# Mixer B's score products: three float32r passes against two 16-bit passes and a half-array remainder

## The chip, the cores and the metric

The kernel runs on one core of one Trainium2 chip, in one launch. The metric is the device time of that launch in microseconds: the median of three runs of the kernel before is 2332.86 us (2331.59 to 2336.87). One further execution, whose time is 2334.11 us, was recorded by the hardware profiler; all rows below are from it.

## The reference

An encoder block over 2048 tokens of width 1024: a norm, one input projection, two attention mixers side by side (A: dilated windows; B: latent attention), an output projection, a mixture of experts, a final norm. All of it is float32. The change is in mixer B, which computes for each of 8 heads

```python
q = (rmsnorm(c_q, g_q_latent) @ w_q_up).reshape(b, s, 8, 64 + 32)     # 64 "nope", 32 rotary
kv = (rmsnorm(c_kv, g_kv_latent) @ w_kv_up).reshape(b, s, 8, 64 + 64) # k_nope, v
k_r = apply_rope(k_rope)                                              # one rotary key for all heads
sc = (q_nope . k_nope + q_rope . k_r) * 96 ** -0.5                    # 2048 x 2048 per head
p = softmax(sc); o = p @ v
```

So each score is a dot product over 96 numbers, of which the last 32 of the key are the same in all heads.

## The kernel before

The block runs in stages on one core: projections (to about 400 us of the span), mixer A (to 703 us), mixer B's preparation (`mla_prep`, 703 to 763 us), mixer B's loop (`mla`, 763 to 1524 us), then output projection, routing and experts.

float32 accuracy on the matrix engine is made by splitting each operand into a high part (float32r, rounded) and a low part (the rest), and adding three products: high x high, high x low, low x high. Each product reads 96 rows of the array (97 where a row with minus the query's maximum rides along) and 512 columns.

`mla` walks over 256 steps `s`: 8 heads x 4 blocks of 512 queries (`m`) x 8 pairs of 128 keys (`kp`). For one step PE does, in this written order: three score products of the first 128 keys (`scores(s, 0)`, L837 to L839), one product of a maximum pass that runs ten steps ahead (`maxpass`, L811, reduced by DVE in L813), three score products of the second 128 keys, another maximum-pass product. After every second step the values of two steps are multiplied in (`pv`, L868 to L873, 36 short float16 products). Now and then comes `mrow` (L821, L822: the finished maxima turned into a row of Qh) or one piece of the next head's k or q (`prep`, L792 to L799; both use the one PSUM bank `X`). ACT takes the exponential of a step's scores twice (L844 to float16 `hi`, L845 to float32 `p32`); their difference `lo` is made by DVE on the first LV = 256 of 512 columns (L850) and by POOL on the rest (L851). The score bank `S` has two buffers, the maximum-pass bank `M` two.

All engines run their queues in program order; the order is written out in the loop `for s in range(NS + 2)`. From step 194 on `ahead5` adds work of the next stage to the same queues, by step number.

`mla_prep` makes, per 128 tokens, the normed latents, q, v, and head 0's k and q. `krows` puts the rotary key into Kh and Kl, which POOL copies for the odd heads' buffers. `pre4` (in mixer A's last units) and `split_c` (in `phase1`) split weights.

Of the kernel before, what the change touches and what calls it, by code (L numbers as in the profile page):

```python
# [12 lines left out]
F32 = mybir.dt.float32  # L13
F32R = mybir.dt.float32r
F16 = mybir.dt.float16
# [7 lines left out]
S, D = 2048, 1024  # L23
# [13 lines left out]
class K:  # L37
# [23 lines left out]
    def consts(self, ctx):  # L61
        nc, tc, io = self.nc, self.tc, self.io
        self.cp = ctx.enter_context(tc.tile_pool(name="consts", bufs=1))
        self.ident = self.cp.tile([128, 128], F32, name="ident")
        make_identity(nc, self.ident)
        self.css = self.cp.tile([128, 2, NT], F32, name="css")
        self.vbs = self.cp.tile([128, 2], F32, name="vb_scale")
        self.RF = self.cp.tile([128, 68], F32, name="rf")
        self.idx = self.cp.tile([128, E], I32, name="eidx")
        self.novf = self.cp.tile([128, 1], I32, name="novf")  # L70
        self.idx2 = self.cp.tile([128, 6], I32, name="eidx2")
        self.glat = self.cp.tile([128, 3], F32, name="glat")
        self.ones = self.cp.tile([128, 128], F32, name="ones")
        nc.gpsimd.memset(self.ones, 1.0)


    def phase1(self):
# [3 lines left out]
        with ExitStack() as ctx:  # L81
# [96 lines left out]

            def split_c(h):
                split(wcv[0][:, 4 * h:4 * h + 4], wcv[1][:, 4 * h:4 * h + 4], wraw[h])  # L180

            stage_a(0)
            split_c(0)
# [37 lines left out]
            def vscale():  # L221

                am = sm.tile([128, 4], F32, name="vmax")
                for i in range(2):
                    nc.scalar.activation(hT[0][:, :, 1792:], raws[i].rearrange("p (j n) -> p j n", j=8), AF.Square, accum_out=am[:, i:i + 1])
                    yield
                nc.vector.tensor_reduce(am[:, 2:3], gb, axis=AX.X, op=ALU.max, apply_absolute_value=True)
                yield
                yield from self.pow2_scale(sm, pt, am, float(D), vsc, dr["va_inv"])

# [205 lines left out]
    def pre4(self, step):  # L436

        nc, io = self.nc, self.io
        f = lambda t: t[:, 0:1536].rearrange("p (k n) -> p k n", k=2)
        if step == 0:  # L440
            self.wq = [f(self.pre.tile([128, S], F32R, name=n)) for n in ("QA16", "KA")]
            self.wqraw = f(self.pre.tile([128, S], F32R, name="KB").bitcast(F32))
            nc.sync.dma_start(self.wqraw, io["w_q_up"][0].rearrange("(k p) n -> p k n", p=128))
            nc.sync.dma_start(self.glat[:, 0:2], io["g_q_latent"][0].rearrange("(k p) -> p k", p=128))
            nc.sync.dma_start(self.glat[:, 2:3], io["g_kv_latent"].rearrange("a p -> p a"))
        else:

            k = step - 1
            g = self.glat[:, k:k + 1]
            nc.scalar.activation(self.wq[0][:, k], self.wqraw[:, k], AF.Copy, scale=g)  # L450
            nc.vector.scalar_tensor_tensor(self.wq[1][:, k], self.wqraw[:, k], g, self.wq[0][:, k],
                                           op0=ALU.mult, op1=ALU.subtract)
# [292 lines left out]
                        put(h // 2, {3: 16, 11: 1, 19: 4}[u])  # L745


    def mla(self):
        nc, tc, io, dr = self.nc, self.tc, self.io, self.dram
        SC = 96 ** -0.5  # L750
        LN64 = math.log(64.0)
        LV = 256
        PASS = ((0, 0), (0, 1), (1, 0))
        with ExitStack() as ctx:
            self.open5()
            pq = ctx.enter_context(tc.tile_pool(name="p4q", bufs=1))
            pp = ctx.enter_context(tc.tile_pool(name="p4", bufs=1))

            names = ("Qh", "Ql", "Kh", "Kl")
            QK = [{n: self.slot(i) for i, n in enumerate(names)}, {n: pq.tile([128, S], F32R, name=n) for n in names}]  # L760
# [5 lines left out]
            sm = ctx.enter_context(tc.tile_pool(name="p4sm", bufs=2))  # L766
            with ExitStack() as c2:
                self.mla_prep(c2, SC, PASS, VB, ckvT, wkv, QK, vsc)
            self.c_pre.close()

            wk = ctx.enter_context(tc.tile_pool(name="p4w", bufs=3))
# [13 lines left out]
            def prep(h, i):  # L785
# [4 lines left out]
                if i % 2 == 0:  # L790
                    for n, (a, b) in enumerate(PASS):
                        nc.tensor.matmul(ps, wkv[b][:, h], ckvT[a][:, sl], start=(n == 0), stop=(n == 2))  # L792
                    nc.scalar.activation(d["Kh"][0:64, sl], ps[0:64], AF.Copy)
                    nc.vector.tensor_sub(d["Kl"][0:64, sl], ps[0:64], d["Kh"][0:64, sl])
                else:
                    for j in range(4):
                        nc.tensor.transpose(ps[0:96, 128 * j:128 * j + 128], qraw[h][:, 4 * n4 + j], self.ident)
                    nc.scalar.activation(d["Qh"][0:96, sl], ps[0:96], AF.Copy, scale=SC)
                    nc.vector.scalar_tensor_tensor(d["Ql"][0:96, sl], ps[0:96], SC, d["Qh"][0:96, sl],  # L799
                                                   op0=ALU.mult, op1=ALU.subtract)  # L800

            def maxpass(m, i):

# [7 lines left out]
                nc.tensor.matmul(ps, d["Qh"][0:96, q0:q0 + 128], d["Kh"][0:96, kc * 512:kc * 512 + 512],  # L811
                                 start=True, stop=True)
                nc.vector.tensor_reduce(part[m][:, qt, kc:kc + 1], ps, axis=AX.X, op=ALU.max)  # L813
                if kc == 3:
# [2 lines left out]
            def mrow(m):  # L817
                h, n = divmod(m, 4)
                ps = psX.tile([128, 512], F32, name="X")
                for qt in range(4):  # L820
                    nc.tensor.transpose(ps[0:97, 128 * qt:128 * qt + 128], mz[m % 2][:, qt], self.ident)  # L821
                nc.vector.tensor_scalar(QK[h % 2]["Qh"][96:97, n * 512:n * 512 + 512], ps[96:97], -1.0, LN64,  # L822
                                        op0=ALU.mult, op1=ALU.add)

            state = {}

            def scores(s, j):
# [6 lines left out]
                ps = state[s][0]  # L834
                k0 = (2 * kp + j) * 128
                kt = slice(k0, k0 + 128)
                nc.tensor.matmul(ps[:, j], d["Kh"][0:97, kt], d["Qh"][0:97, sl], start=True, stop=False)  # L837
                nc.tensor.matmul(ps[:, j], d["Kh"][0:96, kt], d["Ql"][0:96, sl], start=False, stop=False)
                nc.tensor.matmul(ps[:, j], d["Kl"][0:96, kt], d["Qh"][0:96, sl], start=False, stop=True)  # L839
                if j == 1:  # L840
                    hi = wk.tile([128, 2, 512], F16, name="hi", bufs=4)
                    p32 = wk.tile([128, 2, 512], F32, name="p32")
                    lo = wk.tile([128, 2, 512], F16, name="lo", bufs=4)
                    nc.scalar.activation(hi, ps, AF.Exp)  # L844
                    nc.scalar.activation(p32, ps, AF.Exp)  # L845
                    state[s] = (hi, lo, p32)

            def lows(s):
# [70 lines left out]
                    pv(s - 3)  # L919
                    pv(s - 2)  # L920

    def mla_prep(self, ctx, SC, PASS, VB, ckvT, wkv, QK, vsc):
# [15 lines left out]
        calls.update(enumerate(self.c4))  # L938
        nc.gpsimd.memset(kr[:, :, 0:64], 0.0)
        nc.sync.dma_start(kr[:, :, 64:96], AP(dr["c"], 384, [[416, 128], [128 * 416, NT], [1, 32]]))  # L940
        nc.scalar.activation(wkv[0], raw2, AF.Copy, scale=gkv)
        nc.vector.scalar_tensor_tensor(wkv[1], raw2, gkv, wkv[0], op0=ALU.mult, op1=ALU.subtract)
        rs = self.css
# [51 lines left out]
            nc.vector.scalar_tensor_tensor(VB[:, c, :, 65:129], v, vsc, VB[:, c, :, 0:64], op0=ALU.mult, op1=ALU.subtract)  # L995

        def krows(n4):
            ps = pt.tile([128, 4, 128], F32, name="pT")
            for j in range(4):
                nc.tensor.transpose(ps[0:96, j], kr[:, 4 * n4 + j], self.ident)  # L1000
            sl = slice(512 * n4, 512 * n4 + 512)
            src = ps[64:96].rearrange("p a b -> p (a b)")
            d = QK[0]
            nc.scalar.activation(d["Kh"][64:96, sl], src, AF.Copy)
            nc.vector.tensor_sub(d["Kl"][64:96, sl], src, d["Kh"][64:96, sl])
            for n in ("Kh", "Kl"):
                nc.gpsimd.tensor_copy(QK[1][n][64:96, sl], d[n][64:96, sl])

        def kprep(n4):
            sl = slice(512 * n4, 512 * n4 + 512)  # L1010
# [4 lines left out]
            nc.scalar.activation(QK[0]["Kh"][0:64, sl], pf[0:64], AF.Copy)  # L1015
            nc.vector.tensor_sub(QK[0]["Kl"][0:64, sl], pf[0:64], QK[0]["Kh"][0:64, sl])

        def qprep(c):
            if c % 4 == 0:
# [1 line left out]
            ps = qss["ps"]  # L1021
            nc.tensor.transpose(ps[0:96, c % 4], qss.pop(c)[:, 0, 0], self.ident)
            if c % 4 == 3:
                sl = slice(128 * (c - 3), 128 * (c + 1))
                pf = ps.rearrange("p a b -> p (a b)")
                nc.scalar.activation(QK[0]["Qh"][0:96, sl], pf[0:96], AF.Copy, scale=SC)
                nc.vector.scalar_tensor_tensor(QK[0]["Ql"][0:96, sl], pf[0:96], SC, QK[0]["Qh"][0:96, sl],
                                               op0=ALU.mult, op1=ALU.subtract)

        for c in range(2):  # L1030
            stage_a1(c)
        stage_a2(0)
        for c in range(NT):
            if c + 2 < NT:
# [4 lines left out]
            if c >= 1:  # L1039
                qprep(c - 1)  # L1040
            if c == 2:
                for d in QK:
                    nc.gpsimd.memset(d["Kh"][96:97].bitcast(F32), 1.0)
            if c in (4, 6, 8, 10):
                krows(c // 2 - 2)
            if c % 4 == 3:
# [1242 lines left out]
```

## Time and profile before

| | us |
|---|---|
| median of 3 runs | 2332.86 |
| the profiled execution | 2334.11 |
| its span (first to last instruction) | 2332.3 |
| PE busy in the span | 2132.7 (91%) |
| DVE / ACT / POOL busy | 1636.1 / 1361.2 / 1089.9 |
| mixer B's loop, 763 to 1524 us | 761 |

A matmul's record runs from its start to the modelled end of its last column, so records of neighbours overlap: a product is told by the distance from its start to the next one's start, not by its duration. PEld is the loading of weights, which overlaps with PE. The granted clock is a share of 2.4 GHz: 1.00 is the higher level, 0.50 the lower one (1.2 GHz), and values between are means over both.

### The profile page before, as it was taken

How to read it: one execution, taken by the hardware profiler on the slowest of the kernel's cores; microseconds unless marked ns; L12 is line 12 of the kernel's file. 1: busy time of each engine (PE TensorE's matmuls, PEld its weight loads, DVE VectorE, ACT ScalarE, POOL GpSimd, SP SyncE). 2: the span in 40 equal slices, each digit the busy share in tenths (PEclk: the TensorE clock that was granted, in tenths of full speed). 3: DMA queues.
4: the chain of work that ended last, by engine and by line, in shares of the span. 5: the costliest groups of instructions: out<-in, count | busy, mean ns of one | idle time of the engine just before them, and what ended most of it. 6: DMA issues, size and time to landing. Idle time of an engine off the chain costs nothing. (4 is left out here: it accounts for less than half of the span.)

```text
span 2332.3 us, 42859 instructions
## 1 busy us (share of the span) xinstructions
PE 2132.7 (91%) x16077; PEld 1805.7 (77%) x16077; DVE 1636.1 (70%) x3584; ACT 1361.2 (58%) x2103; POOL 1089.9 (47%) x1169
## 2 busy tenths in 40 slices
PE   6899998799999999999999999888888899999990
PEld 5899876699988688888888877776776588788870
DVE  7722111478887788888888898867787677777765
ACT  4522111588887477777777767734433366677653
POOL 1100000366673255555555556654664666667740
PEclk9999999889999899999999999999999999999995
DMA  4312536999955100000000131145534699899978
GB/s 163 126 60 81 193 161 173 208 220 204 206 129 155 36 20 22 6 22 6 22 22 6 27 119 26 34 135 157 153 128 173 195 305 293 292 306 321 307 211 305
DMA packets 196676, 333.79 MB, mean 143 GB/s; under 512 B 64185, under 2 KB 140898, under 8 KB 180388
## 3 DMA queue, kind: packets, MB, share of 16 engines
q1 hardware_dynamic: 166420, 195.41, 29.8%
q0 software_dynamic: 29760, 134.85, 18.0%
q8 instruction: 128, 2.10, 0.4%
q14 instruction: 80, 0.66, 0.1%
q10 hardware_dynamic: 288, 0.79, 0.1%
HBM read 248.24 MB, written 109.64 MB: 153 GB/s over the span
## 5 line engine op out<-in xcount | busy, mean ns | idle before, releaser
L851 POOL TENSOR_TENSOR lo<-p,hi 128x512 f16<-128x512 f32 x256 | 353.5, 1382 | 310.4 <-ACT p L845 308.1
L844 ACT ACTIVATE hi<-S 128x1024 f16<-128x1024 f32 x256 | 261.9, 1023 | 199.1 <-PE S L839 198.9
L813 DVE TENSOR_REDUCE part<-M 128x1 f32<-128x512 f32 x512 | 346.3, 685 | 32.5 <-PE M L811 30.5
L845 ACT ACTIVATE p<-S 128x1024 f32<-128x1024 f32 x256 | 261.0, 1019 | 0.2 <-DVE lo L850 0.2
L850 DVE TENSOR_TENSOR lo<-p,hi 128x512 f16<-128x512 f32 x256 | 218.1, 853 | 7.0 <-ACT p L845 0.2
L873 PE MATMUL O<-VB,lo 128*128 128x65 f16 x2048 | 197.6, 193 | 6.9 <-DVE lo L850 4.6
L868 PEld LDWEIGHTS <-hi 128*128 128x128 f16 x2048 | 182.7, 98 | 24.8 <-issue 23.2
L868 PE MATMUL O<-VB,hi 128*128 128x129 f16 (+1 forms) x2048 | 198.3, 215 | 0.0
L644 POOL TENSOR_TENSOR pp<-sb,st 128x512 f32<-128x512 f32 x32 | 33.5, 1049 | 327.6 <-DVE st L627 312.7
L873 PEld LDWEIGHTS <-lo 128*128 128x128 f16 x2048 | 177.3, 99 | 8.1 <-DVE lo L850 5.4
L650 POOL TENSOR_TENSOR pp<-sb,st 128x256 f32<-128x256 f32 (+1 forms) x256 | 143.0, 580 | 58.7 <-DVE st L627 49.4
L1994 DVE TENSOR_TENSOR s<-raw,s 128x1024 fp32r<-128x1024 f32 x120 | 140.0, 1220 | 16.0 <-ACT s L1992 15.8
L2038 POOL DMA_INDIRECT d_x<-o,rec x47 | 93.5, 1989 | 101.2 <-ACT s L1992 30.7
L1951 PE MATMUL pd<-s,hT 128*128 128x512 f32 x540 | 138.3, 404 | 1.7 <-ACT hT L1938 1.7
L307 DVE SCALAR_TENSOR_TENSOR qk_sb<-pm,qkscale,qk_sb 128x512 fp32r<-128x512 f32 x32 | 24.0, 751 | 163.2 <-ACT qk_sb L306 156.9
L1302 PE MATMUL pm<-s,mT_hi 128*128 128x512 f32 x512 | 134.3, 408 | 0.3 <-ACT mT_hi L1287 0.3
L1992 ACT ACTIVATE s<-raw 128x1024 fp32r<-128x1024 f32 x120 | 118.6, 1051 | 12.5 <-DMA raw<-in_w_gate,eidx 6.0
L1951 PEld LDWEIGHTS pd<-s,hT 128*128 128x128 f32 x540 | 101.0, 188 | 30.3 <-issue 4.3
L602 PE MATMUL S<-KA,QA 128*128 128x256 f32 (+2 forms) x384 | 114.5, 323 | 7.6 <-issue 7.6
L678 ACT ACTIVATE phi<-PT 128x512 f16<-128x512 f32 (+1 forms) x160 | 96.4, 602 | 39.9 <-PE PT L667 38.4
L306 ACT ACTIVATE qk_sb<-pm,qkscale 128x512 fp32r<-128x512 f32 x32 | 22.0, 688 | 167.2 <-DMA d_qk<-qk_sb 115.1
L1302 PEld LDWEIGHTS pm<-s,mT_hi 128*128 128x128 f32 x512 | 96.9, 195 | 21.9 <-ACT mT_hi L1287 0.5
(468 smaller groups left out, 6369.8 us busy)
## 6 DMA issues: line engine op xcount, KB each, us to landing
x<-in_x SPq DMA_DIRECT2D x32, 512.0 KB
d_qk<-qk_sb SPq DMA_DIRECT2D x64, 256.0 KB
na<-d_na SPq DMA_DIRECT2D x48, 264.0 KB
QA<-d_qk SPq DMA_DIRECT2D x16, 512.0 KB
KA<-d_qk SPq DMA_DIRECT2D x16, 512.0 KB
KB<-d_qk SPq DMA_DIRECT2D x16, 512.0 KB
d_x<-x SPq DMA_DIRECT2D x16, 512.0 KB
d_h<-h SPq DMA_DIRECT2D x16, 512.0 KB
```

The source lines that it names most:

```text
L650: nc.gpsimd.tensor_sub(dst, src, res[:, s0 + i, 65:66, None, None].to_broadcast([128, 2, na, nx // 2]))
L813: nc.vector.tensor_reduce(part[m][:, qt, kc:kc + 1], ps, axis=AX.X, op=ALU.max)
L844: nc.scalar.activation(hi, ps, AF.Exp)
L845: nc.scalar.activation(p32, ps, AF.Exp)
L850: nc.vector.tensor_sub(lo[:, :, 0:LV], p32[:, :, 0:LV], hi[:, :, 0:LV])
L851: nc.gpsimd.tensor_sub(lo[:, :, LV:512], p32[:, :, LV:512], hi[:, :, LV:512])
L868: nc.tensor.matmul(o[:, c0:c0 + own], hi[:, j, q], V[:, 0:own], start=(kt == 0 and qt == 0), stop=False, skip_group_check=True)
L873: nc.tensor.matmul(o[:, c0:c0 + 65], lo[:, j, q], V[:, 0:65], start=False, stop=(kt == 15 and qt == 3), skip_group_check=True)
L1302: nc.tensor.matmul(ps[half], mT[a][:, j], wo[b][j // 2][:, j % 2, 512 * half:512 * half + 512], start=(n == 0), stop=(n == 23))
L1951: self.nc.tensor.matmul(ps[:, half], hT[a][:, j], w[b][:, j, 512 * half:512 * half + 512], start=(n == 0), stop=(n == len(k) - 1))
L1992: nc.scalar.activation(hi, src, AF.Copy)
L1994: eng.tensor_sub(lo, src, hi)
```

## The change

q and k of mixer B become float16 high and low halves, after scaling by powers of two that are worked out at run time from sums of squares (`qk_scales`; the squares are summed by added `Square` activations in `split_c`, `pre4` and `mla_prep`). The rows are packed anew:

- K1 (128 rows): k_nope high, k_r high, k_r low; Q1: q_nope high, q_r high, q_r high again. Their product holds three of the terms.
- K2: k_nope low, k_nope high; Q2: q_nope high, q_nope low.
- K3, Q3 (33 rows, kept twice, at partitions 0 and 64): k_r high with q_r low, and a row that carries the maximum. The products of a step's two key tiles use the two halves of the array's rows.

The maximum pass multiplies Q1 and K1 in float16. The copies between partitions are DMAs on SP's queue (one per k piece, five per q piece, five per `krows`); POOL's copies go. The exponential takes its scale and bias from tiles. `mrow` now writes the maxima twice, by DVE and by ACT. LV goes from 256 to 192, so that DVE makes 384 and POOL 640 of a step's 1024 `lo` columns.

```diff
-                nc.tensor.matmul(ps[:, j], d["Kh"][0:97, kt], d["Qh"][0:97, sl], start=True, stop=False)
-                nc.tensor.matmul(ps[:, j], d["Kh"][0:96, kt], d["Ql"][0:96, sl], start=False, stop=False)
-                nc.tensor.matmul(ps[:, j], d["Kl"][0:96, kt], d["Qh"][0:96, sl], start=False, stop=True)
+                nc.tensor.matmul(ps[:, j], d["K1"][:, kt], d["Q1"][:, sl], start=True, stop=False)
+                nc.tensor.matmul(ps[:, j], d["K2"][:, kt], d["Q2"][:, sl], start=False, stop=False)
                 if j == 1:
+                    for i in range(2):
+                        r = slice(64 * i, 64 * i + 33)
+                        nc.tensor.matmul(ps[:, i], K3[r, k0 - 128 + 128 * i:k0 + 128 * i], d["Q3"][r, sl],
+                                         start=False, stop=True)
...
-                    nc.scalar.activation(hi, ps, AF.Exp)
-                    nc.scalar.activation(p32, ps, AF.Exp)
+                    nc.scalar.activation(hi, ps, AF.Exp, scale=es, bias=self.ln64)
+                    nc.scalar.activation(p32, ps, AF.Exp, scale=es, bias=self.ln64)
...
-        LV = 256
+        LV = 192
...
-                nc.vector.tensor_scalar(QK[h % 2]["Qh"][96:97, n * 512:n * 512 + 512], ps[96:97], -1.0, LN64,
-                                        op0=ALU.mult, op1=ALU.add)
+                q3 = QK[h % 2]["Q3"][:, n * 512:n * 512 + 512]
+                nc.vector.tensor_scalar(q3[32:33], ps[96:97], -2.0 ** -15, None, op0=ALU.mult)
+                nc.scalar.activation(q3[96:97], ps[96:97], AF.Copy, scale=-2.0 ** -15)
...
+    def put_q(self, d, ps, sl):
+        nc, sq = self.nc, self.mls[0:96, 0:1]
+        nc.scalar.activation(d["Q1"][0:96, sl], ps[0:96], AF.Copy, scale=sq)
+        ql = self.qlp.tile([128, 512], F16, name="ql")
+        nc.vector.scalar_tensor_tensor(ql[0:96], ps[0:96], sq, d["Q1"][0:96, sl], op0=ALU.mult, op1=ALU.subtract)
+        nc.sync.dma_start(d["Q2"][0:64, sl], d["Q1"][0:64, sl])
+        nc.sync.dma_start(d["Q1"][96:128, sl], d["Q1"][64:96, sl])
+        nc.sync.dma_start(d["Q2"][64:128, sl], ql[0:64])
+        nc.sync.dma_start(d["Q3"][0:32, sl], ql[64:96])
+        nc.sync.dma_start(d["Q3"][64:96, sl], ql[64:96])
...
         for c in range(2):
             stage_a1(c)
+        self.qk_scales(self.sm4, pt)
         stage_a2(0)
...
+            nc.scalar.activation(self.wq[1][:, k], self.wqraw[:, k], AF.Square, scale=g, accum_out=self.mam[:, k:k + 1])
```

`qk_scales` is one small matmul with a matrix of ones and 15 DVE instructions of 1 to 6 columns, each on the result of the one before.

PE's queue in one step of an odd head, before (M is the maximum pass, S the scores):

```order
L837 MATMUL S<-Qh,Kh 128x512
L838 MATMUL S<-Ql,Kh 128x512
L839 MATMUL S<-Qh,Kl 128x512
L811 MATMUL M<-Kh,Qh 128x512
L837 MATMUL S<-Qh,Kh 128x512
L838 MATMUL S<-Ql,Kh 128x512
L839 MATMUL S<-Qh,Kl 128x512
L811 MATMUL M<-Kh,Qh 128x512
```

and the same step now (K_9265 and Q_9267 are K1 and Q1, 9266 and 9268 K2 and Q2, 9270 K3, 9269 Q3):

```order
L853 LDWEIGHTS Q_9267
L853 MATMUL M<-K_9265,Q_9267 128x512
L880 LDWEIGHTS K_9265
L880 MATMUL S<-Q_9267,K_9265 128x512
L881 LDWEIGHTS K_9266
L881 MATMUL S<-Q_9268,K_9266 128x512
L885 LDWEIGHTS K_9270
L885 MATMUL S<-Q_9269,K_9270 128x512
L885 LDWEIGHTS K_9270
L885 MATMUL S<-Q_9269,K_9270 128x512
L853 LDWEIGHTS Q_9267
L853 MATMUL M<-K_9265,Q_9267 128x512
```

Two float32r products of every step (L839) have become two 33-row products side by side in the queue (L885), after the second key tile's K2 product and ahead of the second maximum-pass product; the weight loads now stand as instructions of their own.

DVE's queue at the start of `mla_prep`, before (`s` and `t` are slots of weights):

```order
L942 SCALAR_TENSOR_TENSOR s_9261<-t_8740,glat,s_9261 128x1024
L965 TENSOR_TENSOR cqT_lo<-pT,cqT_hi 128x256
L966 TENSOR_TENSOR s_9260<-pT,s_9259 128x128
L965 TENSOR_TENSOR cqT_lo<-pT,cqT_hi 128x256
L966 TENSOR_TENSOR s_9260<-pT,s_9259 128x128
```

and now (5 of the 15 instructions of `qk_scales`, the first two, one in the middle and the last two, are shown with what stands ahead and behind):

```order
L1008 SCALAR_TENSOR_TENSOR s_9273<-t_8749,glat,s_9273 128x1024
L766 COPY qks<-pT 128x6
L768 TENSOR_TENSOR qks<-qks 128x1
...
L771 TENSOR_SCALAR qks<-qks,mla_norms 128x1
...
L782 TENSOR_SCALAR qks<-qks 128x2
L783 TENSOR_SCALAR mla_scale<-qks 128x1
L1031 TENSOR_TENSOR cqT_lo<-pT,cqT_hi 128x256
```

The chain stands between the split of the kv weights and the first `cqT_lo`, for which PE waits.

## Rows read from the trace of the kernel before

**Rows 1.** Stretches of the span: busy us (count) per engine, clock, DMA share, GB/s.

```profile
703.00:763.10 60.10, 57.28 (x343) 52.54 (x340) 42.11 (x124) 46.36 (x109) 24.19 (x45) 1.00 0.61 161
781.20:1380.00 598.80, 598.40 (x5740) 501.13 (x5740) 510.32 (x872) 441.71 (x504) 317.01 (x262) 1.00 0.07 20
1380.00:1524.00 144.00, 129.96 (x1219) 102.17 (x1219) 129.38 (x195) 102.72 (x127) 92.23 (x76) 0.93 0.17 54
```

**Rows 2.** Groups by line and form, PE, mixer B's loop: busy us, mean ns.

```profile
L837 PE MATMUL S<-Qh,Kh 97*128 97x512 f32 x256 | 109.2, 426 | 0.3 <-ACT p L845 0.2
...
L838 PE MATMUL S<-Ql,Kh 96*128 96x512 f32 x256 | 102.8, 402 | 0.0
L797 PE MATMUL X<-ident,s 128*96 128x128 f32 x112 | 16.8, 272 | 0.0
```

**Rows 3.** Timeline of PE, 1000 to 1007 us: start, us, line, tiles.

```profile
1000.25 0.40 PE L837 MATMUL S<-s,s 97*128 97x512 f32 x1
...
1002.12 0.86 PE L792 MATMUL X<-s,s 128*128 128x512 f32 x3
1002.82 0.23 PE L868 MATMUL O<-VB,hi 128*128 128x129 f16 x1
1002.89 0.19 PE L873 MATMUL O<-VB,lo 128*128 128x65 f16 x1
...
1004.21 0.19 PE L873 MATMUL O<-VB,lo 128*128 128x65 f16 x1
1004.24 0.51 PE L837 MATMUL S<-s,s 97*128 97x512 f32 x1
1004.58 0.41 PE L838 MATMUL S<-s,s 96*128 96x512 f32 x1
```

**Rows 4.** Timeline of PE in `phase1`, around 33-row products, about 76.5 us.

```profile
76.27 0.60 PE L153 MATMUL pT<-ident,xn 128*128 128x128 f32 x4
76.80 0.34 PE L401 MATMUL pT<-hT_hi 33*8 33x384 f32 x1
```

**Rows 5.** The same, about 50.5 us.

```profile
50.47 0.42 PE L401 MATMUL pT<-hT_hi 33*8 33x496 f32 x1
50.73 0.42 PE L402 MATMUL pT<-hT_hi 33*8 33x496 f32 x1
51.08 0.65 PE L163 MATMUL pm<-wc_hi,hT_hi 128*128 128x416 f32 x2
```

**Rows 6.** Groups by line and form, DVE, ACT and POOL, mixer B's loop.

```profile
L813 DVE TENSOR_REDUCE part<-M 128x1 f32<-128x512 f32 x512 | 346.3, 685 | 32.5 <-PE M L811 30.5
L850 DVE TENSOR_TENSOR lo<-p,hi 128x512 f16<-128x512 f32 x256 | 218.1, 853 | 7.0 <-ACT p L845 0.2
...
L844 ACT ACTIVATE hi<-S 128x1024 f16<-128x1024 f32 x256 | 261.9, 1023 | 199.1 <-PE S L839 198.9
L798 ACT ACTIVATE Qh<-X 96x512 fp32r<-96x512 f32 x16 | 9.5, 595 | 0.0
...
L851 POOL TENSOR_TENSOR lo<-p,hi 128x512 f16<-128x512 f32 x256 | 353.5, 1382 | 310.4 <-ACT p L845 308.1 <-PE O L873 1.0 <-DVE lo L850 0.6
```

**Rows 7.** Timeline at the start of `mla_prep`, PE and DVE.

```profile
705.25 1.31 PE L960 MATMUL pT<-ident,cn 128*128 128x128 f32 x6 [1.91 <-ACT cn L951]
707.30 0.51 PE L976 MATMUL pq<-QA,cqT_lo 128*128 128x384 f32 x2
...
704.88 1.28 DVE L942 SCALAR_TENSOR_TENSOR s<-t,glat,s 128x1024 fp32r<-128x1024 f32 x1 [2.09 <-ACT s L941]
706.64 0.42 DVE L965 TENSOR_TENSOR cqT_lo<-pT,cqT_hi 128x256 fp32r<-128x256 f32 x1 [0.47 <-ACT s L964]
```

**Rows 8.** Timeline of DVE in `phase1`: dependent instructions of one column.

```profile
17.02 0.15 DVE L48 TENSOR_SCALAR rs_t<-rs_t 128x1 int32<-128x1 int32 x1
17.21 0.15 DVE L49 TENSOR_SCALAR rs_t<-rs_t 128x1 int32<-128x1 int32 x1
```

**Rows 9.** One line, ACT, in `pre4`: ns min/median/max, first and last start us.

```profile
L450 ACT ACTIVATE QA<-KB,glat x2: 987/988/988, 683.0 to 684.8; 128x768 fp32r<-128x768 f32 x2
```

More of the change, by code (lines that the diff above doesn't have):

```diff
@@ L72, in consts @@
         self.glat = self.cp.tile([128, 3], F32, name="glat")
+        self.mam = self.cp.tile([128, 6], F32, name="mla_norms")
+        self.mls = self.cp.tile([128, 3], F32, name="mla_scale")
+        self.ln64 = self.cp.tile([128, 1], F32, name="ln64")
+        nc.gpsimd.memset(self.ln64, math.log(64.0))
         self.ones = self.cp.tile([128, 128], F32, name="ones")
@@ L180, in split_c @@
                 split(wcv[0][:, 4 * h:4 * h + 4], wcv[1][:, 4 * h:4 * h + 4], wraw[h])
+                cj = cev.tile([128, 256], BF16, name="c_junk")
+                nc.scalar.activation(cj[:, 0:128].rearrange("p (j n) -> p j n", j=4), wraw[h][:, :, 384:416], AF.Square,
+                                     accum_out=self.mam[:, 3 + h:4 + h])
             stage_a(0)
@@ L745, in phase3, with qk_scales @@
                         put(h // 2, {3: 16, 11: 1, 19: 4}[u])
+    def qk_scales(self, sm, psp):
+        nc = self.nc
+        V = nc.vector
+        t = sm.tile([128, 16], F32, name="qks", bufs=1)
+        ps = psp.tile([128, 4, 128], F32, name="pT")
+        nc.tensor.matmul(ps[:, 0, 0:6], self.ones, self.mam, start=True, stop=True)
+        V.tensor_copy(t[:, 0:6], ps[:, 0, 0:6])
+        g = self.mam[:, 5:6]
+        V.tensor_add(t[:, 6:7], t[:, 0:1], t[:, 1:2])
+        V.tensor_scalar(t[:, 6:7], t[:, 6:7], 256.0, None, op0=ALU.mult)
+        V.tensor_add(t[:, 7:8], t[:, 3:4], t[:, 4:5])
+        V.tensor_scalar(t[:, 7:8], t[:, 7:8], g, g, op0=ALU.mult, op1=ALU.mult)
+        V.tensor_scalar(t[:, 7:8], t[:, 7:8], 8.0, None, op0=ALU.mult)
+        V.tensor_add(t[:, 7:8], t[:, 7:8], t[:, 2:3])
+        V.tensor_scalar(t[:, 7:8], t[:, 7:8], 128.0, None, op0=ALU.mult)
+        V.tensor_scalar(t[:, 8:10], t[:, 6:8], 1e-30, 1e30, op0=ALU.max, op1=ALU.min)
+        ti = t.bitcast(I32)
+        V.tensor_scalar(ti[:, 8:10], ti[:, 8:10], 1, None, op0=ALU.logical_shift_right)
+        V.tensor_scalar(ti[:, 8:10], ti[:, 8:10], float(127 << 22), None, op0=ALU.add)
+        V.tensor_single_scalar(ti[:, 10:12], ti[:, 8:10], 0x7F800000, op=ALU.bitwise_and)
+        V.tensor_scalar(self.mls.bitcast(I32)[:, 0:2], ti[:, 10:12], -1.0, float((127 + 14 + 127) << 23),
+                        op0=ALU.mult, op1=ALU.add)
+        V.tensor_scalar(ti[:, 12:14], ti[:, 10:12], -float(14 << 23), None, op0=ALU.add)
+        V.tensor_scalar(self.mls[:, 2:3], t[:, 12:13], t[:, 13:14], 96 ** -0.5, op0=ALU.mult, op1=ALU.mult)
     def mla(self):
         nc, tc, io, dr = self.nc, self.tc, self.io, self.dram
-        SC = 96 ** -0.5
-        LN64 = math.log(64.0)
-        LV = 256
+        LV = 192
         PASS = ((0, 0), (0, 1), (1, 0))
@@ L757, in mla @@
             pp = ctx.enter_context(tc.tile_pool(name="p4", bufs=1))
-            names = ("Qh", "Ql", "Kh", "Kl")
-            QK = [{n: self.slot(i) for i, n in enumerate(names)}, {n: pq.tile([128, S], F32R, name=n) for n in names}]
+            names = ("K1", "K2", "Q1", "Q2", "Q3")
+            half = [self.slot(i, F16) for i in range(3)]
+            QK = [{n: half[i // 2][:, S * (i % 2):S * (i % 2) + S] for i, n in enumerate(names)},
+                  {n: pq.tile([128, S], F16, name=n) for n in names}]
+            K3 = pq.tile([128, S], F16, name="K3")
+            sq, sk, es = (self.mls[:, i:i + 1] for i in range(3))
             ckvT = [self.slot(4), self.slot(5)]
@@ L1002, in krows @@
             src = ps[64:96].rearrange("p a b -> p (a b)")
[L1003 to L1007, printed above, removed]
+            sk = self.mls[64:96, 1:2]
+            hi, lo = QK[0]["K1"][64:96, sl], QK[1]["Q2"][64:96, sl]
+            nc.scalar.activation(hi, src, AF.Copy, scale=sk)
+            nc.vector.scalar_tensor_tensor(lo, src, sk, hi, op0=ALU.mult, op1=ALU.subtract)
+            for d in QK:
+                nc.sync.dma_start(d["K1"][96:128, sl], lo)
+            for t, r in ((K3, 0), (K3, 64), (QK[1]["K1"], 64)):
+                nc.sync.dma_start(t[r:r + 32, sl], hi)
         def kprep(n4):
@@ L1041, in mla_prep @@
             if c == 2:
[L1042 to L1043 removed]
+                for r in (32, 96):
+                    nc.gpsimd.memset(K3[r:r + 1], 2.0 ** 15)
             if c in (4, 6, 8, 10):
```

32 lines of the change are left out of this document (16 added, 16 removed).

## The prediction

> **What bounds the kernel now.** I read the busy time by stretches first, then the groups of mixer B's loop, then its timeline. In the stretches the reader is to see one long piece, 781 to 1380 us, in which PE is busy 598.40 of 598.80 us at the full clock, while DVE has 510, ACT 442 and POOL 317 us [rows 1]. PE is the bound there, and what one step costs is what PE needs for it. The other engines' waits agree: nearly all of ACT's idle time in front of the exponential (198.9 us) ends with the last score product, and POOL's with ACT [rows 6]. Only in 1380 to 1524 us does PE leave time, 14 of 144 us; there the next stage's work crowds DVE (129.38 of 144). So every ns that PE saves in a step is worth nearly 256 ns, until DVE is full.
>
> PE's own unit is the distance between starts. From 1000.25 to 1002.12 stand eight float32r products of 512 columns, 1.87 us, so 234 ns each [rows 3]. A step has eight of them, six for scores and two for the maximum pass. The value products of two steps, 36 float16 ones, start at 1002.82 and end where the next step starts, 1004.24: 1.42 us [rows 3].
>
> **The change part by part.**
>
> *Six full products per step in float16 instead of float32r.* No row shows a float16 product of 512 columns. The 36 short ones move 4 x 776 = 3104 columns in 1.42 us. Read as 2.4 columns per ns (the granted clock is 1.00 there, rows 1) plus a fixed price, that is 1293 ns and 3.5 ns for each; 512 columns then take 217 ns. Read as a price per column alone it is 0.457 ns, and 512 columns take 234 ns, as in float32r. Below 213 ns no reading goes. I take 217, because in the same rows a product of 129 columns (0.07 to the next) and one of 65 (0.03) stand in no worse proportion than their columns. Gain 17 x 6 = 102 ns a step, between 0 and 126.
>
> *The third pair becomes two 33-row products.* Before, the pair cost 2 x 234 = 468 ns. The two new ones use different halves of the array's rows and write different banks. No row of this case shows two such products at once: together they cost between one product (217) and two (434). I take one, plus 30 ns by which the second weight load follows the first (the short products' loads follow each other at about that distance, 0.03 us from 1004.21 to 1004.24) [rows 3].
>
> What a switch between the full array and part of it costs is shown in `phase1`, where products of 33 rows stand among full ones. Going in: four full transposes start at 76.27 and take 0.60 us together; one alone takes 0.27 [rows 2], so they are 0.11 apart, the last starts at 76.60, and the next full one could start at 76.71. The 33-row product starts at 76.80, 0.09 later [rows 4]. Coming out: two 33-row products are 0.26 apart (50.47, 50.73), the full product behind them comes after 0.35, again 0.09 later [rows 5]. Behind the switch a weight load isn't hidden: the float32r product behind the value products needs 0.34 instead of 0.234 to its successor (1004.24, 1004.58), the first float16 product behind a float32r one 0.07, where 129 / 2.4 + 3.5 make 0.057 [rows 3]. So per step two switches of 90 ns and two open float16 loads of 10 ns (0 to 100 each): 200 ns. The pair now: 217 + 30 + 200 = 447 ns, a gain of 21 ns; the bounds are a gain of 251 (both at once, no price for switching) and a loss of 350 (434 and 384 for the switches).
>
> The Trainium skill speaks against this part (TensorEngine Tiling (Array Packing), Key Properties): changing the tiling mode, not just the tile, drains the engine. The rows agree, with 0.09 us each way. The same skill (TensorE: Matmul & The Clock Gate, Part 3) has products in different row groups start 4 ns apart, and (same page, Part 1, on the 56 ns gap) gives N / 2.4 GHz + 2.5 ns for a warm product, 215.7 ns at 512 columns; by these two figures the sum below would be some (26 + 7 x 1.3) x 256 ns = 9 us better. No row here shows either.
>
> *The open weight load behind value products and transposes.* All float32r products of a loop have the same width, but L837, the first of each three, lasts 426 ns in the mean against 402 for L838 [rows 2]: 24 ns x 512 = 12.3 us in all, since its load stands open behind the value products (the 1004.24 row). In float16 the first one pays 10 ns in some 160 places: a gain of 10.7 us, 0 to 12.
>
> *Work that moves between the other engines.* DVE's `lo` share falls from 512 to 384 columns, 853 x 0.25 = 213 ns a step less; POOL's grows from 512 to 640, 1382 x 0.25 = 345 ns a step more, to about 1.9 us a step with its two `os` operations, of some 2.7 [rows 6]. Both stay beside PE. ACT gains one copy of one row per block, at most 595 ns [rows 6] in 8 steps. DVE's balance per step improves, so I count no new wait for the bank M.
>
> *Costs.* (a) `qk_scales`: 15 dependent DVE instructions at 0.19 us (17.02, 17.21) [rows 8] are 2.9 us, in DVE's queue ahead of the first `cqT_lo`, which was made at 706.64 and which PE needed at 707.30 [rows 7]; the added `Square` ahead of the kv split shifts ACT, DVE and PE by another 0.5 us or so. PE has a quarter of a microsecond of slack, and behind it the preparation is PE-bound (57.28 of 60.10 us) [rows 1]: 3.5 us, between 0 and 5. (b) Two more `Square` activations of 0.99 us on ACT at the end of mixer A [rows 9], and two small ones in `phase1`: 1.5 us, between 0 and 3. (c) `mrow`'s ACT copy stands behind two exponentials of 1 us [rows 6], and the bank X is held until then. Where `prep` follows in the next step (14 places) PE may wait some 0.3 us: 4 us, between 0 and 8. (d) In 1380 to 1524 us part of the gain has no bound to work on: 2 us. (e) The DMAs: one to five a piece, on SP's queue, some steps ahead of their use (pieces are ready by step 15 of a head, the next head's scores begin at 32, its maximum pass at 22), and the DMA engines are at 0.07 [rows 1]. Queued behind them on SP are the output blocks and the next q, which nobody waits for in that time: 0. In `mla_prep` the same DMAs stand between the loads of c, which are issued four chunks ahead: 0, up to 3. The last two also hold a gain that I don't count: POOL loses eight copies there.
>
> *The sum.* Gain: (102 + 21) x 256 = 31.5 us, and 10.7, so 42. Costs: 3.5 + 1.5 + 4 + 2 = 11. The profiled execution took 2334.1 us (span 2332.3 and 1.8 around it), 1.2 over the median of the runs; 2334.1 - 31 = 2303 us. Against the median the same sum gives 2302; I say 2303.
>
> **The rivals.**
>
> *The two halves run one after the other (slower).* The array's halves can be used by turns and not at once: the second product starts when the first is through. For it: PE's products are in one queue, and no row shows two at once. Against it: they share neither rows nor banks nor weights. Then the pair costs 217 - 30 = 187 ns more a step, 48 us: 2351 us. It decides from a start-to-start distance of about 150 ns within the pair upwards: there the gain of 31 is gone.
>
> *No price for the switch.* The 33-row products of `phase1` also have only 8 output columns, so the 0.09 us could be theirs and not the row split's. Then 200 ns a step fall away, 51 us: 2252 us.
>
> *Columns cost the same in both types.* By the other reading of the value products a 512-column float16 product takes 234 ns. Then seven products a step lose 17 ns each, 30 us: 2333 us, no change. For it: the short products alone can't tell. Against it: they would then have no fixed price at all.
>
> *Long open loads at the switches.* If a float16 load behind a switch costs what a float32r one does (0.34 - 0.234 = 0.1 us), two of them cost 51 us in place of 5: 2349 us. Half of that gives 2326.
>
> **How the numbers follow.** Chances: the forecast with its smaller terms (2285 to 2323 us) 0.5; halves by turns 0.18; no price for the switch 0.1; equal columns 0.1; long loads 0.12. A run of this kernel can tell 0.2%, 4.7 us, from no change. The forecast, the cheap switch and half of the long loads are faster: 0.66. No change is what equal columns give, about 0.1 with what overlaps from its neighbours. Slower: the halves by turns and the worse half of the long loads, 0.24. The range reaches from just above the cheap switch, 2262, to the halves by turns, 2352; it leaves out about 2 in 10. The likeliest case's own range is 2285 to 2323.
>
> **What would show it.** In the timeline of the new loop: full products 217 ns apart (234 would be the equal columns); the two 33-row products within 0.05 us of each other (0.2 means by turns); 0.31 us from the second key tile's K2 product to the first 33-row one and from the last of them to the next full product (0.22 would mean a free switch, 0.4 and more an open load). The loop from the first score product on should take some 30 us less than 743, and the preparation 3 us more. The prediction is wrong if PE is no longer the bound, say with DVE waiting for POOL's share of `lo`, or if PE waits for the bank X or M by more than 10 us in all.

## The result and the profile after

The changed kernel takes 2352.41 us (median of 5 runs, 2348.96 to 2355.70) where the kernel before takes 2331.59 (2328.31 to 2336.87): a ratio of 1.0089, 95% interval 1.0068 to 1.0110. It is slower by 0.9%. Forecast were 2303 us. Three executions of the programs below took 1.4 to 3 times as long as their neighbours and stand in no ratio.

The profiled execution has a span of 2353.9 us, 21.6 more than before. First the stretches that answer to [rows 1]: the preparation and the loop up to 1380 us. The columns are the same.

```profile
705.40:774.30 68.90, 61.78 (x335) 55.71 (x336) 44.99 (x139) 47.45 (x111) 19.49 (x37) 0.93 0.65 163
789.50:1380.00 590.50, 565.53 (x5637) 311.14 (x5636) 473.44 (x858) 526.15 (x522) 355.80 (x257) 1.00 0.13 33
```

Three things are to be seen. PE, which left 0.4 us of 599 idle before, now leaves 25 of 590. ACT went from 442 to 526 us of busy time in a stretch that is 8 us shorter. And the preparation takes 68.9 us where it took 60.1. From the first score product to the last value product the loop took 742.9 us before (781.15 to 1524.0) and takes 751.4 now (789.47 to 1540.9), where 30 us less were forecast. With the starts of the `hi` exponential read 32 steps apart, a step takes 2.827 us; it took 2.815. (Step times below are read in the same way, from the middle heads.)

The groups by line and form of the whole loop say whose work grew. POOL's subtraction went from 353.5 to 411.2 us, as its larger share made likely; DVE's fell from 218.1 to 190.4. ACT's exponential, which answers to L844 in [rows 6], grew too:

```profile
L890 ACT ACTIVATE hi<-S,ln,mla_scale 128x1024 f16<-128x1024 f32 x256 | 308.1, 1204 | 63.5 <-PE S L885 62.0
```

The exponential went from 1023 to 1204 ns (the second one, L891, to 1201). Its inputs tell why, and the experiments confirm it: beside S it now reads `ln` (the bias tile `ln64`) and `mla_scale` (the scale tile). Two exponentials a step make 0.36 us more on ACT, 92 us over the loop. The idle time ahead of it fell from 199 to 63 us: ACT used up the room that it had.

How that reaches PE is in the timeline around 1002 us (start, us, engine, line):

```profile
1000.34 1.21 ACT L891 ACTIVATE p<-S,ln,mla_scale 128x1024 f32<-128x1024 f32 x1
...
1001.25 0.38 PE L880 MATMUL S<-s,s 128*128 128x512 f16 x1
...
1001.42 0.68 ACT L971 ACTIVATE K<-X,mla_scale 64x512 f16<-64x512 f32 x1
1001.46 0.38 PE L881 MATMUL S<-s,s 128*128 128x512 f16 x1
...
1002.12 0.38 PE L881 MATMUL S<-s,s 128*128 128x512 f16 x1
...
1002.14 0.74 DVE L972 SCALAR_TENSOR_TENSOR K<-X,mla_scale,K 64x512 f16<-64x512 f32 x1 [1.40 <-ACT K L971]
...
1002.42 0.39 PE L885 MATMUL S<-s,K 33*128 33x512 f16 x2
...
1002.75 0.39 PE L853 MATMUL M<-s,s 96*128 96x512 f16 x1
...
1002.86 1.20 ACT L890 ACTIVATE hi<-S,ln,mla_scale 128x1024 f16<-128x1024 f32 x1 [0.32 <-PE S L885]
...
1002.97 0.38 PE L880 MATMUL S<-s,s 128*128 128x512 f16 x1
...
1003.14 0.69 DVE L855 TENSOR_REDUCE part<-M 128x1 f32<-128x512 f32 x1
...
1003.19 0.38 PE L881 MATMUL S<-s,s 128*128 128x512 f16 x1
...
1003.88 0.38 PE L853 MATMUL M<-s,s 96*128 96x512 f16 x1 [0.31 <-DVE part L855]
...
1005.05 1.20 ACT L890 ACTIVATE hi<-S,ln,mla_scale 128x1024 f16<-128x1024 f32 x1
```

Read it from ACT on. The copy of the next head's K (L971) stands in ACT's queue behind the two long exponentials and begins at 1001.42. DVE's half of that piece (L972) has waited 1.40 us for it, and the maximum of M behind it in DVE's queue has waited too. So the bank M comes free late, and PE stops 0.31 us at 1003.88; from start to start that is 0.69 us (from 1003.19), where 0.22 is usual. ACT for its part has waited 0.32 us for scores at 1002.86. Each engine has idle time, and still the step is longer: the three wait for each other in turn.

Why ACT's room in the mean did not help can be read from the short steps, those without value products. PE needs 1.72 us for one (1001.25 to 1002.97; it needed 1.87 before). ACT's two exponentials need 2.19 (1002.86 to 1005.05), where they fitted into 1.86 before. So ACT falls behind in every second step, and what it has room for lies in the steps with value products.

PE's waits in 785 to 1380 us (in total, times, longest) are

```profile
PE M L853 <- DVE part L855: 12.8, 29, 1.3
PE X L841 <- ACT s L866: 4.8, 8, 0.6
PE X L841 <- ACT Q L866: 3.6, 6, 0.6
```

and 1.2 us for scores. In the kernel before they are 0.3 us in all. L866 is `mrow`'s copy on ACT.

The same rows show that PE's own part came out as worked out: full products 0.21 to 0.22 us apart, the two 33-row products merged into one row (x2, 0.39 us, no longer than one product; their starts are 3 to 4 ns apart in the trace), 0.30 us into the pair and 0.33 out of it. The pair with its switches is 0.63 - 0.217 = 0.41 us; forecast were 0.447.

In the preparation one wait is there that the kernel before does not have (waits of ACT, 705 to 774 us: in total, times, longest):

```profile
ACT qs L1050 <- DMA d_q<-qs: 8.7, 4, 3.4
```

ACT can't write the next `qs` since the store of q from that buffer, one of two, isn't through.

### The profile page after: what moved, and what is told of

Its sections match the earlier page's. It is cut to its first block, busy times and chain, and to the rows that moved or that the text cites. A ratio compares the mean times of both kernels' runs of the same rounds, so it can differ in the third digit from the quotient of the medians.

```text
span 2353.9 us, 43062 instructions
## 1 busy us (share of the span) xinstructions
PE 2105.5 (89%) x16079; PEld 1587.8 (67%) x16079; DVE 1607.5 (68%) x3600; ACT 1477.9 (63%) x2145; POOL 1140.9 (48%) x1162
## 5 line engine op out<-in xcount | busy, mean ns | idle before, releaser
L897 POOL TENSOR_TENSOR lo<-p,hi 128x640 f16<-128x640 f32 x256 | 411.2, 1611 | 252.9 <-ACT p L891 202.2
L855 DVE TENSOR_REDUCE part<-M 128x1 f32<-128x512 f32 x512 | 340.7, 681 | 21.2 <-PE M L853 19.8
L890 ACT ACTIVATE hi<-S,ln,mla_scale 128x1024 f16<-128x1024 f32 x256 | 308.1, 1204 | 63.5 <-PE S L885 62.0
L891 ACT ACTIVATE p<-S,ln,mla_scale 128x1024 f32<-128x1024 f32 x256 | 307.5, 1201 | 0.3 <-DVE lo L896 0.3
L896 DVE TENSOR_TENSOR lo<-p,hi 128x384 f16<-128x384 f32 x256 | 190.4, 744 | 21.1 <-ACT p L891 19.7
L661 POOL TENSOR_TENSOR pp<-sb,st 128x256 f32<-128x256 f32 (+1 forms) x256 | 143.0, 580 | 63.6 <-DVE st L638 56.6
L853 PE MATMUL M<-K,Q 96*128 96x512 f16 x256 | 99.2, 387 | 19.1 <-DVE part L855 17.5
```

What stands on the lines that cost most here:

```text
L661: nc.gpsimd.tensor_sub(dst, src, res[:, s0 + i, 65:66, None, None].to_broadcast([128, 2, na, nx // 2]))
L890: nc.scalar.activation(hi, ps, AF.Exp, scale=es, bias=self.ln64)
L891: nc.scalar.activation(p32, ps, AF.Exp, scale=es, bias=self.ln64)
L896: nc.vector.tensor_sub(lo[:, :, 0:LV], p32[:, :, 0:LV], hi[:, :, 0:LV])
L897: nc.gpsimd.tensor_sub(lo[:, :, LV:512], p32[:, :, LV:512], hi[:, :, LV:512])
```

## The experiments

The theories named in the expectations: A, the tiles of the exponentials make ACT, and what waits behind it, the bound; B, the copies around the max row and the next head's preparation hold the loop; C, the pair of 33-row products does. All ratios are to the kernel before, run on the same chip, with the 95% interval; e1 to e4, e5 to e8, e9 to e11 and e12 ran on four chips. Each trace is one execution.

**e1_immediate.** The scale as a number, the bias tile kept:

```
-  nc.scalar.activation(hi, ps, AF.Exp, scale=es, bias=self.ln64)
+  nc.scalar.activation(hi, ps, AF.Exp, scale=ES, bias=self.ln64)   # ES = 96 ** -0.5 / 1024; p32 the same
```

> The changed kernel with one edit: the two exponentials take their scale as a number written into the instruction (96^-0.5/1024, what the tile holds for these inputs) and no longer from the scale tile. Theory A (the scale tile makes ScalarE the bound of the loop): an exponential of 1024 columns falls from 1.20 to about 1.02 us, the loop's step from 2.826 to 2.66-2.71 us, the time by 30 to 42 us, to 2310-2322. Theory B (ScalarE's and VectorE's copies around the max row and the next head's preparation hold the loop) and theory C (the pair of 33-row products holds it): the exponentials get shorter, but the step stays above 2.79 us and the time above 2343.

Ratio 1.0001 (0.9984 to 1.0018): all that was lost is back, and none of the gain is there. The exponential takes 1.11 us and the step 2.738: between A and its rivals, since half the added price stayed. A's number was wrong: it had put the whole 0.18 us on the scale tile. The written number holds for these inputs only, here and in e5 to e9; e10 lifts that.

**e2_before_tile.** The kernel before, with a scale tile that holds 1.0:

```
-  nc.scalar.activation(hi, ps, AF.Exp)
+  nc.scalar.activation(hi, ps, AF.Exp, scale=self.one1)   # p32 the same
```

> The kernel before with one edit: its two exponentials take a scale of 1.0 from a tile. Theory A: an exponential goes from 1.02 to about 1.20 us there too, 0.36 us a step on ScalarE; the step of 2.815 us, which TensorE filled to the last 0.1%, now has both engines near their limits, and the time rises by 5 to 25 us, to 2337-2357. Theories B and C: ScalarE is still under the step's 2.815 us by its busy time (2.10 + 0.36 us), so the time moves by less than 3 us.

Ratio 1.0028 (1.0011 to 1.0045), the step 2.842 us where it was 2.815. The tile alone slows a kernel whose PE was full, though ACT still idles 124 us ahead of the exponential in 785 to 1380 us. Its price, 1023 to 1113 ns, is 0.09 us and not 0.18:

```profile
L846 ACT ACTIVATE hi<-S,one 128x1024 f16<-128x1024 f32 x209 | 232.6, 1113 | 124.1 <-PE S L841 124.1
```

**e3_mrow_dve.** The max row's second copy on DVE:

```
-  nc.scalar.activation(q3[96:97], ps[96:97], AF.Copy, scale=-2.0 ** -15)
+  nc.vector.tensor_scalar(q3[96:97], ps[96:97], -2.0 ** -15, None, op0=ALU.mult)
```

> The changed kernel with one edit: the second copy of the max row (row 96 of Q3) is written by VectorE, where ScalarE wrote it. Theory B: ScalarE's copy and the bank that it held go out of the way, 32 times 0.3 to 0.5 us: the time falls by 10 to 16 us. Theory A: ScalarE loses 32 copies of 0.6 us, VectorE, on which TensorE also waits, gains them: the time stays within 6 us of the changed kernel's. Theory C: no change.

Ratio 1.0076 (1.0058 to 1.0093), the step 2.828 us: no change in the loop, so B's forecast fails. The edit doesn't take the wait away, though: PE's waits for the bank X are 10.2 us in 13 places here, ended by DVE, where they were 8.4 us in 14, ended by ACT. What tells A from B is e1 and e5.

**e4_const_scales.** Constants in place of the measured scales (the four Squares and `qk_scales` left out).

> The changed kernel without the measuring of the scales: no Squares, no qk_scales, the three scales are constants set at the start (16, 64, 96^-0.5/1024, the values that the kernel finds for these inputs). The loop is untouched. If the chain of one-column operations on VectorE is what moved the first score product from 781.2 to 789.5 us, it comes back to 783-786 and the time falls by 3 to 7 us; if the new DMAs on SyncE's queue moved it (stores of q waited for, 8.7 us in ScalarE's waits), the first score stays above 786 and the time falls by less than 3 us.

Ratio 1.0061 (1.0040 to 1.0082), which overlaps the changed kernel's: a gain of some 6 us is possible and not shown. Its trace has a granted clock of 0.56 throughout the loop, so no place in it can be compared.

**e5_no_tiles.** e1, and ln 64 back in the max row, as in the kernel before:

```
-  nc.vector.tensor_scalar(q3[32:33], ps[96:97], -2.0 ** -15, None, op0=ALU.mult)
+  nc.vector.tensor_scalar(q3[32:33], ps[96:97], -2.0 ** -15, LB, op0=ALU.mult, op1=ALU.add)
   # row 96 the same by bias=LB; LB = log(64) / ES * 2.0 ** -15; no bias in the exponentials
```

> The kernel of e1_immediate with a second edit: ln 64 goes back into the max row (a number added in the two copies of mrow), so that the exponentials have neither a scale tile nor a bias tile, as in the kernel before. e1 took off half of the added time of an exponential (1.20 to 1.11 us) and half of the forecast gain. Theory A (the two tiles cost about 0.09 us each per exponential, and ScalarE with the copies that wait behind it holds the loop): an exponential takes 1.02 us, the step falls from 2.738 to 2.67-2.70 us, the ratio to the kernel before from 1.000 to 0.993-0.997. Rival (what is left in e1 is held by VectorE's and GpSimd's chain behind the exponentials, or by TensorE itself): the step stays above 2.725 us and the ratio above 0.998.

Ratio 0.9951 (0.9934 to 0.9968), faster than before. The exponential takes 1027 ns, the step 2.683 us. The group of the exponential in e5:

```profile
L892 ACT ACTIVATE hi<-S 128x1024 f16<-128x1024 f32 x218 | 223.9, 1027 | 107.3 <-PE S L887 106.7
```

The stretch 900 to 1300 us (columns as in [rows 1]), in which PE of the changed kernel is busy 383.23 us:

```profile
900.00:1300.00 400.00, 396.02 (x4094) 223.20 (x4094) 349.94 (x617) 324.51 (x373) 251.01 (x187) 1.00 0.12 31
```

PE is the bound again, 99% busy, with 396.02 / 400 x 2.683 = 2.656 us of work a step. The prediction's terms (102 + 21 ns, and 10.7 us over 256 steps) had made 2.815 - 0.165 = 2.650. That the two are so close is in part luck: with the pair at the 0.41 us that it takes, the same terms make 2.616, and the busy time counts the records' tails at each wait. A holds, and it is the loop's loss: the step is 2.827, 2.738 and 2.683 us with two, one and no tile, and in most of the short steps the starts of `hi` are 2.19, 2.01 and 1.83 us apart.

**e6_scales_later.** e5 with `qk_scales` behind the second chunk's products:

```
-        self.qk_scales(self.sm4, pt)
         stage_a2(0)
...
+            if c == 1:
+                self.qk_scales(self.sm4, pt)
```

> The kernel of e5_no_tiles with qk_scales moved from ahead of the first chunk's transposes to behind the second chunk's products (its results are first read at the fourth chunk). If the chain of one-column operations stopped TensorE at the start of the preparation (5.4 us busy of 8 at 706-714 us, its clock at 0.58 there, where it was 1.00 before), the hole goes and the time falls by 3 to 7 us against e5. If the store of the old results and the DMAs set that start, it falls by less than 2 us.

Ratio 0.9917 (0.9901 to 0.9933), some 6 to 8 us under e5 as hoped. But its trace doesn't show the reason: the first maximum product comes at 773.3 us against 773.7, and the hole in PE's work at 706 to 714 us is still there (5.96 us busy, clock 0.58). The trace is of e6's slowest execution, 2315.23 us with a median of 2310.56, and e5's, of 2314.68, is under its median of 2316.17, so that the two could hardly show it. Why the time fell is left open.

**e7_qs4.** e6 with `qs` in four buffers (`bufs=4` for `bufs=2`).

> The kernel of e6_scales_later with four buffers for qs, where there were two. If ScalarE's waits for the stores of q (8.7 us in 4 waits, which the kernel before does not have there) come from the new DMAs ahead of the stores on SyncE's queue, the preparation gets 5 to 9 us shorter and the time falls by as much against e6. If the DMA engines themselves are the limit there, or the waits only move to the chunks' loads on the same queue, it falls by less than 2 us.

Ratio 0.9895 (0.9877 to 0.9913), some 5 us under e6, with intervals that overlap. ACT's wait for the stores is gone:

```profile
ACT qs L1052 <- DMA d_q<-qs: 0.2, 1, 0.2
```

The first maximum product comes at 760.8 us, against 773.3 in e6, but that is not all the buffers' work. The traces differ in where the preparation starts: mixer A's last product ends at 697.4 us in e7 and at 705.4 in e6, and between 696.6 (e12) and 707.8 (e8) in all, in a part of the kernel that these edits hardly touch (703.3 and 699.2 in the kernel before and in e2). So the preparation has to be measured from there to the first maximum product. With two buffers it takes 68.9 us (the changed kernel), 69.5, 70.2, 69.2, 67.9 and 67.8 (e1, e3, e5, e6, e8), with four 63.4, 63.6, 62.4, 63.6 and 63.0 (e7, e9 to e12), and 59.7 and 61.0 in the kernel before and e2 (the 60.1 above is from 703.0 on). So the two buffers cost five to six of the nine microseconds; three stay, and what they are is open. That the stores come late because they stand behind the new DMAs on SP's queue is likely, but not shown: four buffers hide a late store whatever made it late. The hole goes with the start of the preparation: e9 has it at 706 to 714 us (clock 0.59), e7 and e12 at 698 to 706 (0.57).

**e8_full_rows.** e5 with the remainder on all rows, zeros in the unused ones:

```
-  nc.tensor.matmul(ps[:, i], K3[r, k0 - 128 + 128 * i:k0 + 128 * i], d["Q3"][r, sl], ...
+  nc.tensor.matmul(ps[:, i], K3[:, k0 - 128 + 128 * i:k0 + 128 * i], d["Q3"][:, sl], ...
```

(POOL fills K3 and Q3 with zeros ahead of it, and `krows` has one DMA less.)

> The kernel of e5_no_tiles with the 33-row remainder as two products over all 128 rows (the other rows of K3 and Q3 hold zeros), so that the array is never split and nothing is gained by two at once. From the trace of the changed kernel the pair takes 0.63 - 0.217 = 0.41 us of TensorE with its two switches; two full products take 0.434. If the pair is worth only what that leaves, the step changes by +0.02 us at most and the time by -3 to +6 us against e5. Theory C (the weight loads that wait 0.42 us for issue ahead of each pair are lost time): the time falls by over 12 us.

The step is 2.704 us against 2.683: 0.02 more, which is 0.434 - 0.413. C falls, and with it the waits "issue" ahead of the pair's weight loads (88.6 us) as a loss. The time can't tell 5 us: 0.9928 (0.9910 to 0.9945), if anything below e5's. So the split array, for all its rows and copies, is worth 0.02 us of 2.68 a step; nearly all of PE's gain is the float16 pace.

**e9_lv128, e10_fixed_product, e12_lv256.** From e7: less of `lo` on DVE (`LV = 128`); then q's scale as 1024 over k's, so that the written number holds for any k, without the Squares of q's weights; then that with `LV = 256`.

> The kernel of e7_qs4 with LV = 128: VectorE subtracts 256 columns of each low half where it did 384, GpSimd 768 where it did 640. In e7 VectorE is busy 88% of the loop and TensorE waits for its maxima 9 to 11 us of 595; the exponentials no longer wait. If VectorE is now the engine behind which TensorE waits, the step falls from 2.683 to 2.64-2.665 us and the time by 4 to 10 us. If GpSimd (62% busy, 1.54 us an operation, then about 1.85) is late for the low products instead, the time rises by 2 us or more.

> The kernel of e9_lv128 with only k's scale found from the norms and q's set to 1024 over it, so that the exponentials' written scale holds for any k; the two Squares over q's weights and a few one-column operations go. The chain is off TensorE's way already and ScalarE has room where the Squares stand: within 3 us of e9; up to 4 us less if the Squares (some 0.8 us each) stood on the path.

> The kernel of e10_fixed_product with LV = 256, the kernel before's split of the low halves (512 columns each on VectorE and GpSimd). In e9 and e10 VectorE's subtraction of 256 columns took 867 ns where 384 columns took 806 in e7: fewer columns, more time. If its time is set by GpSimd's operation beside it and not by its own columns, 512 columns take 800 to 840 ns, GpSimd's operation falls to about 1.38 us, the step is 2.67-2.69 us and the ratio 0.987-0.992, as good as e7. If the columns decide, VectorE gets over 900 ns, TensorE's waits for the maxima double, and the ratio is above 0.994.

e9: 0.9950 (0.9929 to 0.9971), the step 2.694 us; e10: 0.9929 (0.9911 to 0.9947), 2.693; e12: 0.9891 (0.9871 to 0.9911), 2.700. Both bets on `LV` were wrong in the loop. (e9's time lies above e7's, as its second theory said, but not for that theory's reason: PE waits for POOL's low products 2.8 us in all, 2.5 in e7, and 8.5 of the 14.8 us between the two traces lie ahead of the preparation.) DVE's subtraction doesn't follow its columns. The groups of 820 to 1380 us, e7 with 384 columns on DVE,

```profile
L898 DVE TENSOR_TENSOR lo<-p,hi 128x384 f16<-128x384 f32 x206 | 168.9, 820 | 0.0
```

e9 with 256,

```profile
L898 DVE TENSOR_TENSOR lo<-p,hi 128x256 f16<-128x256 f32 x205 | 177.6, 867 | 1.2
```

and e12 with 512:

```profile
L894 DVE TENSOR_TENSOR lo<-p,hi 128x512 f16<-128x512 f32 x206 | 197.3, 958 | 0.0
```

(POOL's subtraction takes 1544, 1717 and 1325 ns in the three.) 256 columns take longer than 384, and in the changed kernel 384 took 705 in the same stretch. Taking columns off DVE doesn't shorten it here. e12's time is as low as e7's with the longest of the three steps. Its trace is 12.3 us shorter than e10's: 5.2 us of it lie ahead of the preparation, in code that both share, and 8.5 us in the stretch from step 192 to the last value product, where the next stage's work runs beside (195.0 us for 203.4). With `LV = 192` that stretch took 197.9 to 201.1 us (e5 to e8), with 128 in e9 201.7; so `LV` may matter there, which one trace each doesn't settle.

**e11_prep_only.** The changed kernel, tiles kept, with e6's and e7's edits.

> The changed kernel, both tiles of the exponentials kept, with only the two edits of the preparation: qk_scales behind the second chunk and four buffers for qs. If the losses of the preparation and of the loop are separate and add up, the first maximum comes at about 761 us where it came at 774, the step stays at 2.826 us, and the ratio to the kernel before is 1.002 to 1.006 (e7's gain on e5, 0.0056, taken from 1.0089). If the loop gives the earlier start back, or the preparation's loss hangs on the loop, the ratio stays above 1.007.

Ratio 1.0055 (1.0035 to 1.0075), the preparation 63.6 us, step 2.827. The two losses are separate and add up, as far as these intervals can tell.

e7 and e12 beat both kernels, by 1.0 and 1.1% against the one before: 25 and 26 us, where 31 were forecast for the change.

## Why the prediction was wrong

The step that failed is the balance of ACT: "ACT gains one copy of one row per block". The exponentials' new scale and bias tiles were not in it. The runs show 1204 ns for each exponential in place of 1023, 0.36 us more of ACT a step; without the tiles (e5) the step falls from 2.827 to 2.683 us. The new call stands in the diff, and the page of the kernel before has the price, in two rows of ACT with 512 columns each:

```profile
L678 ACT ACTIVATE phi<-PT 128x512 f16<-128x512 f32 (+1 forms) x160 | 96.4, 602 | 39.9 <-PE PT L667 38.4
L306 ACT ACTIVATE qk_sb<-pm,qkscale 128x512 fp32r<-128x512 f32 x32 | 22.0, 688 | 167.2 <-DMA d_qk<-qk_sb 115.1
```

With a scale tile 0.086 us more (0.083 with L678's 128x512 form alone, 605 ns). Twice that on two exponentials is 0.34 us a step, and 1023 + 172 = 1195 ns would have been near the 1204 measured. The Trainium skill has it too (ScalarE: Activation LUTs, What ACT_TABLE_LOAD costs): some 93 ns for each pointer operand of 128x1. The runs agree: 1027, 1113 and 1204 ns with none, one and two.

Point by point. *Float16 products*: right, 0.217 us apart, no equal columns. *The pair*: right in its mechanism, both at once (not by turns) with a price for each switch; 0.41 us for 0.447. (The bound of 384 ns for its switches is 380 by its own terms, which changes nothing.) *The open load*: right in the timeline, where the K1 product behind the value products is followed after 0.21 us (1001.25, 1001.46; 0.215 in the median of 102 places) and the float32r one was after 0.34 (0.319 in the median); the step times are not fine enough to show its 10.7 us. *No new wait for the bank M*: wrong, 12.8 us of PE's waits between 785 and 1380 us, where the kernel before has 0.3. Two thirds of it stay in e5 (9 us), where ACT is out of the way; with DVE 87% busy there, I put those on DVE's queue, which was not tried by itself. *POOL's share*: 1611 ns, under the 1727 worked out, and hardly ever late (3 us of the waits for the low products end with it). *DMAs at 0, up to 3 us*: wrong in the preparation, five to six us, because with them ACT waits for the stores of q, which have only two buffers (e7). *qk_scales at 3.5 us*: the chain took its 2.8 us (708.82 to 711.64); what it cost in time is not settled (e4, e6). *mrow's copy at 4 us*: right in the wait, in the 14 places named, with 0.6 us each for 0.3: 8.4 us, above the bound of 8. It is 2.3 us in e5, where ACT is earlier, so most of it is the exponentials' doing; moving the copy (e3) took neither the wait nor the time away.

In the sum: the forecast's step of 2.650 us and the measured 2.827 are 0.177 us apart, 45 us over 256 steps, where the forecast had 6 us of its costs, (c) and (d); the first maximum came 11.2 us late where 5 were counted (2 of the 11 lie ahead of the preparation, where traces of the same code differ by more). That is 45 of the 52.6 us between the forecast (31 less) and the span (21.6 more). Of the rest, 4 us are the steps 190 to 221, beside the next stage's work (3.172 for 3.055 us), and 5 the part behind the loop (813 for 808 us), which I did not follow, and the first maximum pass gives 3 back (15.2 for 18.1 us). The prediction itself named what would sink it, PE no longer being the bound. The neighbour that it named for that, DVE waiting for POOL, was the wrong one; its other sign, more than 10 us of waits for the banks X and M, came (21.2 us). For ACT, the third neighbour, it worked out no price.

## What to carry to other kernels

When a change takes work off the engine that is the bound, write down for every other engine each instruction that gets another form, with operands and not only with columns; the room that these engines had is a sum over a step and not a guarantee, since a copy that queues behind two longer instructions arrives late at once (e2: ACT's busy time had room, and the time rose). A scale that is known when the kernel is written belongs into the instruction, and a constant shift into data that is written anyway; e10 shows how a measured scale can be made such a number. New DMAs beside stores from a double buffer can cost time though nobody waits for the new ones: here five to six us, which two more buffers took away. And a place in one trace, like the start of a stage, is to be compared from the end of the stage ahead, since that alone moved by up to 11 us between these traces.

## What was not expected of the hardware

- An activation pays about 0.09 us for each tile that it takes its scale or bias from (1027, 1113, 1204 ns for 1024 columns).
- Two products of 33 rows in different halves of the array run at once and take no longer together (0.39 us in one row) than one; into and out of the split the distances are 0.30 and 0.33 us in the rows shown (0.31 and 0.32 in the median of 208) where 0.217 is the full product's. With that, the pair beats two full products by 0.02 us only.
- DVE's subtraction with both inputs in SBUF took 665 (384 columns, e3) to 958 ns (512, e12) with no order by columns (867 for 256), always beside POOL's subtraction. The Trainium skill (SBUF — State Buffer, Who interferes with whom) says that such an instruction waits for a GpSimd one that reads SBUF, and the other way round. No run here had DVE's without POOL's beside it, so it is neither shown nor refuted.
